# Gate projections moved among the SSD projections and kept in DRAM until their branch is merged

## The chip, the cores and the metric

The kernel runs on one core of one Trainium2 chip. The metric is device time in microseconds (us) of one launch, the median of several runs. The float32 products are made from three matmuls on rounded halves (high times high, high times low, low times high), so every weight block has to be split into a high and a low part before TensorE can use it.

## The reference, cut to what matters

Two layers, sequence of 512, model width 1024. What the change touches is one layer's mixing half:

```python
h = rmsnorm(x, norm_mix_g[l])
proj = h @ w_in[l]                      # 14384 columns: GLA, SSD, differential attention, 3 x 1024 gate logits
y_gla = gla_mixer(...)                  # 4 heads, chunked recurrence
y_ssm = ssd_mixer(z, xbc, dt, ...)      # 4 groups: conv of width 4 + silu on x, B, C; scan; y * silu(z); group rms norm
y_diff = diff_mixer(...)                # 8 heads, two softmaxes each
gates = sigmoid(gate_logits + b_gate).reshape(bsz, s_len, 3, D_MODEL)
mixed = gates[0] * (y_gla @ w_br_gla) + gates[1] * (y_ssm @ w_br_ssm) + gates[2] * (y_diff @ w_br_diff)
x = x + mixed @ w_out[l]
```

It is followed by a squared-ReLU MLP with 4096 hidden columns, a residual add, and after both layers a final norm.

## The kernel before, in words

All activations lie transposed, 128 channels on the partitions and 512 tokens in the free dimension. The unit of TensorE work is an *item*: one block of 128 output columns with all 1024 input channels (`item_a`, L867). It loads one weight block of 512 KB into a `wraw` tile (two buffers), splits it in two halves into `whi` (ScalarE copy) and `wlo` (VectorE or GpSimd subtraction), and issues 24 matmuls of 512 columns into one PSUM bank `d`. Then its `fin` takes the result from PSUM. `item_a2` (L893, for the SSD branch) gives two 128-column outputs from 512 channels, `item_w` (L942) a 512-column output with the tokens on the partitions; they are built of the same half blocks.

The order of the work is made at build time by a planner (`Flow`). Items stand in one list. `refill` (L373) keeps six half blocks queued: it walks the first `AHEAD` items of the list and takes the first whose buffers (`need`) and conditions (`cond`, `when`) are met on the planner's own clock. All the small work (scans, softmaxes, norms) is in *tasks*, generators that yield what they wait for; a ready task goes before the next matmul of an item. The planner's clock uses fixed costs per instruction (`Model.cost`, L153), and each engine's instructions, and the DMA issues of the one queue on SyncE (SP), are emitted in the order of that clock. On the chip each of these streams runs in order, so an instruction that waits holds what is behind it.

Items of a layer stand in the list in this order: the first pair of GLA heads; four SSD groups; the second pair of GLA heads; the SSD branch product of the last group; six `item_w` for the two halves of the differential attention; eight gates of the SSD branch; then per branch (GLA, then differential) gates and products interleaved, a gate two or four places ahead of its product; then the output projection and the MLP.

An SSD group (`ssd_group`, L1125) lists B, C, x0 to x3, z0 to z3. B, C and x go through `conv` (L1111): one ScalarE pass, three VectorE passes of 512 columns, a ScalarE tanh, one more VectorE pass. A z block costs one ScalarE and one VectorE pass. Then come the four `item_a2` that project the group before it (`ssm_part`, L1804). The group's tasks (`chunk`, `state`, `finish`) start when its convolutions are there; each `chunk` fetches decay rows from DRAM by the SP queue (`tw<-acs`, `tt<-acs`). `pj` has ten buffers and a group holds six.

A gate (`gate_item`, L1793) ends with one tanh from PSUM into a `tt` tile, which is held until the VectorE pass that multiplies it in. The SSD gates (`ssm_gates`, L1828) wait for the whole SSD sum, the others (`branch`, L1841) for a product that is so many places ahead.

Of the kernel before, what the change touches and what calls it, by code (L numbers as in the profile page):

```python
# [12 lines left out]
F32 = mybir.dt.float32  # L13
# [4 lines left out]
ALU = mybir.AluOpType  # L18
# [4 lines left out]
P = 128  # L23
S = 512
D = 1024
NT = S // P
KT = D // P
DEPTH = 2
# [6 lines left out]
O_Z, O_X, O_B, O_C, O_DT = 3088, 5136, 7184, 7696, 8208  # L35
O_CQ, O_CK, O_CV, O_GATE = 8240, 9264, 10288, 11312

C_CONVW, C_CONVB = 0, 96
C_MIX, C_MLP, C_BG, C_GK, C_DN, C_SN = 120, 128, 136, 160, 164, 165
N_COLS = 181  # L40

# [18 lines left out]


HOP = 0.22
SLACK, LAG, BACK, AHEAD = 0.4, 0.15, 6.0, 16
POOL_MARGIN = 0.5
QN = 6
LEAD = 2
# [584 lines left out]
class Trunk:  # L651
# [37 lines left out]
    def setup(self):  # L689
        nc, a, tc = self.nc, self.a, self.tc  # L690
        c = self.const
        self.ident = c.tile([P, P], F32, name="ident")
        make_identity(self.tc.nc, self.ident)
        self.ones = c.tile([P, P], F32R, name="one_row")
        self.one_row = self.ones.bitcast(F32)
        nc.gpsimd.memset(self.one_row, 1.0)
        self.xt_dram = [self.dram.tile([KT, P, S], F32, name=f"xt{l}") for l in range(DEPTH)]
        self.low_dram = [self.dram.tile([16, S], F32, name=f"low{l}") for l in range(DEPTH)]
        self.ac_dram = [self.dram.tile([32, S], F32, name=f"acs{l}") for l in range(DEPTH)]
        self.cols = [c.tile([P, N_COLS], F32, name=f"cols{l}") for l in range(DEPTH)]  # L700
        self.fcol = c.tile([P, KT], F32, name="fcol")
        self.masks = c.tile([P, 5, 16], U8, name="masks")
        self.ident32 = c.tile([P, 32], F32, name="ident32")
        self.cos = c.tile([P, NT, 8], F32, name="cos")
        self.sin = c.tile([P, NT, 8], F32, name="sin")
# [149 lines left out]
        self.act(hi, x, AF.Copy)  # L855
        self.sub(lo, x, hi)

    def item(self, blocks, start, body, fin, acts, cond, chain):
        def end(it):
            fin(it)  # L860
            acts.done()
        acts.users += 1
        it = Item(blocks, start, body, end, cond, acts.when, chain)
        self.f.items.append(it)
        return it
# [27 lines left out]
    def item_a2(self, w, k0, m0, acts, fin, extra=(), cond=()):  # L893
        f = self.f

        def body(it, i, wt):
            wh, wl = wt
            for j in range(2):
                k = i * 2 + j
                ah, al = acts.get(k)  # L900
                for u in range(2):
                    cs = slice(u * P, (u + 1) * P)
                    ps = it.held[u].ap
                    yield None
                    f.mm(ps, wh[:, j, cs], ah, k == 0, False)
                    f.mm(ps, wh[:, j, cs], al, False, False)
                    f.mm(ps, wl[:, j, cs], ah, False, k == 3)

        src = w[k0 * P:(k0 + 4) * P, m0 * P:(m0 + 2) * P]
        return self.item(Block(self, [src], 4, 256).parts(), [("d", ([P, 512],))] * 2 + list(extra),  # L910
                         body, fin, acts, cond, False)

    def item_pair(self, srcs, acts, fin):

# [207 lines left out]
        self.act(th, acc, AF.Tanh)  # L1122
        nc.vector.scalar_tensor_tensor(acc, th, 1.0, acc, op0=ALU.add, op1=ALU.mult)

    def ssd_group(self, l, g, h, evdt, quads, evy, before=None):  # L1125
        nc, a, f = self.nc, self.a, self.f
        w = a["w_in"][l]
        V, G = nc.vector, nc.gpsimd
# [15 lines left out]
                ev.t = f.at(it.held[1].ap)  # L1144
            self.item_a([w[:, c0:c0 + P]], h, fin, extra=pj, chain=False)

        conv_item(O_B + g * P, 16 + g, "b", st["evb"])
        conv_item(O_C + g * P, 20 + g, "c", st["evc"])
        for m in range(4):
            conv_item(O_X + g * 512 + m * P, g * 4 + m, m, st["evx"][m])  # L1150

        def z_item(m):
            def fin(it):
                if m % 2 == 0:
# [6 lines left out]
            c0 = O_Z + g * 512 + m * P  # L1161
            self.item_a([w[:, c0:c0 + P]], h, fin, extra=() if m % 2 else [("z4", ([P, 2, S],))],
                        cond=st["evz"][m - 1] if m % 2 else ())
        for m in range(4):
            z_item(m)

        def prep():
            yield ([st["evb"], st["evc"]] + ([before["evt"]] if before else []), {"m": 1, "tt": 4})
# [621 lines left out]
            f.spawn(head(hh))  # L1790


    def gate_item(self, l, br, m, h, cont, cond=()):  # L1793
        cb = C_BG + br * 8 + m

        def fin(it):
            ps, g = it.held
            self.act(g.ap, ps.ap, AF.Tanh, scale=0.5, bias=self.cols[l][:, cb:cb + 1])
            ps.free()
            cont(g)  # L1800
        self.item_a([self.a["w_in"][l][:, O_GATE + br * D + m * P:O_GATE + br * D + (m + 1) * P]], h, fin,
                    extra=[("tt", ([P, S],))], cond=cond).need["tt"] = 4

    def ssm_part(self, l, g, ev, quads, merged, evm):  # L1804
        V, f = self.nc.vector, self.f
        w = self.a["w_br_ssm"][l]
        acts = Acts(lambda j: self.part([quads[g]], j), last=lambda: self.drop([quads[g]]))
        left = [4]

        def fin_of(m0):  # L1810
            def fin(it):
                for i in range(2):
                    ps = it.held[i]
                    if g == 0:
                        merged[m0 + i] = it.held[2 + i]
                        self.act(merged[m0 + i].ap, ps.ap, AF.Copy)
                    else:
                        m = merged[m0 + i].ap
                        V.tensor_tensor(m, m, ps.ap, op=ALU.add)
                    ps.free()  # L1820
                left[0] -= 1
                if left[0] == 0:
                    evm.t = f.clock
            return fin
        for m0 in range(0, KT, 2):
            self.item_a2(w, g * 4, m0, acts, fin_of(m0), extra=[("res", ([P, S],))] * 2 if g == 0 else (), cond=ev)

    def ssm_gates(self, l, h, merged, evm, gated):  # L1828
        V, f = self.nc.vector, self.f

        def cont_of(m):
            def cont(g):
                x = merged[m].ap
                V.scalar_tensor_tensor(x, g.ap, 1.0, x, op0=ALU.add, op1=ALU.mult)
                g.free()
                gated[m].t = f.clock
            return cont
        for m in range(KT):
            self.gate_item(l, 1, m, h, cont_of(m), cond=evm)

    def branch(self, l, br, name, slots, evs, h, merged, gated, lead, final=None, gone=None):  # L1841
        V, f = self.nc.vector, self.f
        w = self.a[name][l]

        def drop():
            self.drop([s[0] for s in slots])
            if gone:
                gone.t = f.clock
        acts = Acts(lambda k: self.part([slots[k // 4][0]], k % 4),
                    last=drop)  # L1850
        made = [Event() for _ in range(KT)]
        taken = [Event() for _ in range(KT)]
        gs = [None] * KT

        def gate(m):
            def cont(g):
                gs[m] = g
                made[m].t = f.clock
            self.gate_item(l, br, m, h, cont, cond=taken[m - lead] if m >= lead else ())

        def prod(m):
            def fin(it):
                g = gs[m]
                V.scalar_tensor_tensor(g.ap, g.ap, 1.0, it.held[0].ap, op0=ALU.add, op1=ALU.mult)
                it.held[0].free()
                self.tt(merged[m].ap, merged[m].ap, g.ap, ALU.add)
                g.free()
                if final:
                    f.spawn(final(m))

            def hook(it):
                taken[m].t = f.clock
            it = self.item_a([w[:, m * P:(m + 1) * P]], acts, fin, cond=[*evs, made[m], gated[m]])
            it.hook = hook
        for m in range(KT + lead):
            if m < KT:
                gate(m)
            if m >= lead:
                prod(m - lead)


    def layer(self, l, ns, more):
# [22 lines left out]
                        lambda it: f.spawn(self.dt_task(l, it.held[0], evdt)), cols=48)  # L1905
        self.gla_duo(l, 0, h, gs[0], evg, dt_item)
        st = None
        for g in range(4):
            st = self.ssd_group(l, g, h, evdt, quads, evy[g], st)
            if g == 3 and l == 0:  # L1910
                late = Event()
                f.spawn(self.rope_tables(late))
                f.items[-1].hook = lambda it: setattr(late, "t", f.clock)
            if g > 0:
                self.ssm_part(l, g - 1, evy[g - 1], quads, merged, evm[g - 1])
        self.gla_duo(l, 1, h, gs[1], evg, before=[st["evt"]])
        self.ssm_part(l, 3, evy[3], quads, merged, evm[3])
        gone = Event()
        for duo in range(2):
            self.diff_duo(l, duo, h, ds[duo], evd[duo], gone if duo else None)  # L1920
        self.ssm_gates(l, h, merged, evm[3], gated)
        mq = [None, None]
        ma = Acts(lambda k: self.part(mq, k), [Event() for _ in range(KT)], lambda: self.drop(mq))

        def merge(m):
# [7 lines left out]
            nc.vector.scalar_tensor_tensor(lo, x.ap, 0.5, hi.bitcast(F32), op0=ALU.mult, op1=ALU.subtract)  # L1933
            x.free()
            ma.when[m].t = f.at(hi, lo)
        self.branch(l, 0, "w_br_gla", gs, evg, h, merged, gated, 2, gone=gone)
        self.branch(l, 2, "w_br_diff", ds, evd, h, merged, gated, 4, merge)
        cols = self.cols[l]
        n2 = Normed(self, cols[:, C_MLP:C_MLP + 8], 32, False)
        xn = n2.xs  # L1940
# [238 lines left out]
```

## Time and profile before

| | us |
|---|---|
| median of 3 runs (2815.11 to 2816.82) | 2815.18 |
| the profiled execution: its time | 2813.3 |
| the profiled execution: span of its instructions | 2811.4 |
| TensorE matmul busy | 2730.2 (97%) |
| VectorE busy | 1787.6 (64%) |
| ScalarE busy | 1313.6 (47%) |
| GpSimd busy | 560.9 (20%) |
| mean granted TensorE clock | 0.987 |

The chain of work that ended last is 89% TensorE and 6% VectorE. The span falls into stages that repeat in both layers: the first pair of GLA heads and the norm (to about 150 us), SSD groups with the second pair of GLA heads in their tail (about 200 to 650 and 1500 to 2000 us), differential attention with the GLA branch (650 to 950, 2000 to 2300), the differential branch and the output projection, and the MLP (1050 to 1400, 2430 to the end). Matmuls are pipelined, so a busy TensorE isn't a TensorE at its peak: the number of matmuls in a stretch says more than its busy time.

### The profile page before, as it was taken

Reading aid. Unit: us, or ns where it says so; the run is one execution under the profiler, and the core shown is the slowest. Engines: PE = TensorE matmul, PEld = TensorE weight load, DVE = VectorE, ACT = ScalarE, POOL = GpSimd, SP = SyncE. Lnnn points to the kernel's source line nnn. Section 1 sums busy time; section 2 is a strip of 40 time slices with the busy share of each in tenths; the row PEclk is TensorE's granted clock in tenths of the full one; section 3 lists DMA queues with packets and bytes.
Section 4 is the critical chain, followed back from the end, with each engine's and each line's share of the span. In section 5 each row is a group of like instructions: output and inputs, shape, how many; then the busy total and the mean of one; then the engine's idle time right before and its main releaser. Section 6 shows DMA issues by size and latency. Waiting matters only on the chain.

```text
span 2811.4 us, 40467 instructions
## 1 busy us (share of the span) xinstructions
PE 2730.2 (97%) x14956; PEld 2234.8 (79%) x14956; DVE 1787.6 (64%) x3804; ACT 1313.6 (47%) x2646; POOL 560.9 (20%) x620
## 2 busy tenths in 40 slices
PE   8998799999999999999999999899999999999998
PEld 6777587878888888888877778687888888888887
DVE  6787578864778455444478876778666754544445
ACT  5664545543656333223346656545365633332222
POOL 3323321331221001011013233333132100021001
PEclk9999899999999999999999999999999999999999
DMA  4343334223222343333343434332222233333332
GB/s 145 93 106 85 103 102 112 85 81 98 68 76 68 90 128 92 98 98 98 98 125 81 115 104 109 105 104 76 83 75 76 76 83 99 119 98 98 98 98 83
DMA packets 434818, 268.72 MB, mean 96 GB/s; under 512 B 15078, under 2 KB 407900, under 8 KB 434620
## 3 DMA queue, kind: packets, MB, share of 16 engines
q1 hardware_dynamic: 434004, 265.08, 33.7%
q8 instruction: 117, 1.92, 0.3%
q10 hardware_dynamic: 616, 1.06, 0.1%
q14 instruction: 81, 0.66, 0.1%
HBM read 259.62 MB, written 6.49 MB: 95 GB/s over the span
## 4 chain that ended last, share of the span: by engine, by line
PE 89%; DVE 6%; ACT 2%; DMA 1%; issue 1%; SPq 0%; DVEq 0%; ACTq 0%
PE d L367 79%; PE m L367 8%; PE m L371 3%; DVE tt L80 2%; DVE pj L80 1%; DVE wlo L80 1%; ACT tw L80 1%; DVE hl L80 1%; DVE rs_t L80 0%; ACT whi L80 0%; ACT cth L80 0%; DVE z L80 0%; DVE rs_y L80 0%; DMA z<-in_x 0%; DMA tt<-acs 0%
## 5 line engine op out<-in xcount | busy, mean ns | idle before, releaser
L367 PE MATMUL d<-hl,whi 128*128 128x512 f32 (+2 forms) x5696 | 1783.8, 395 | 24.4 <-ACT whi L80 19.6
L367 PEld LDWEIGHTS d<-hl,whi 128*128 128x128 f32 (+1 forms) x5696 | 1052.8, 189 | 240.0 <-ACT whi L80 22.5
L367 PE MATMUL d<-hl,wlo 128*128 128x512 f32 (+2 forms) x2848 | 1114.0, 391 | 15.4 <-DVE wlo L80 15.4
L80 ACT ACTIVATE whi<-wraw 128x512 fp32r<-128x512 f32 x868 | 541.0, 628 | 1050.6 <-PE d L367 958.2
L80 DVE TENSOR_TENSOR wlo<-wraw,whi 128x512 fp32r<-128x512 f32 (+1 forms) x807 | 587.7, 735 | 549.9 <-ACT whi L80 539.3
L367 PEld LDWEIGHTS d<-hl,wlo 128*128 128x128 f32 (+1 forms) x2848 | 536.8, 188 | 134.9 <-DVE wlo L80 21.2
L367 PE MATMUL d<-whi,hl 128*128 128x512 f32 x1280 | 410.8, 402 | 8.0 <-DVE z L80 5.8
L80 POOL TENSOR_TENSOR tt<-tt 128x512 f32<-128x512 f32 x128 | 159.5, 1255 | 983.9 <-ACT hl L80 857.1
L367 PEld LDWEIGHTS d<-whi,hl 128*128 128x128 f32 x1280 | 233.6, 190 | 55.2 <-DVE z L80 7.4
L367 PE MATMUL d<-wlo,hl 128*128 128x512 f32 x640 | 252.4, 394 | 0.0
L80 POOL TENSOR_TENSOR wlo<-wraw,whi 128x512 fp32r<-128x512 f32 (+1 forms) x61 | 79.5, 1304 | 360.0 <-ACT whi L80 255.7
L367 PEld LDWEIGHTS d<-wlo,hl 128*128 128x128 f32 x640 | 121.5, 190 | 26.7
L80 DVE TENSOR_TENSOR res<-res,d 128x512 f32<-128x512 f32 (+1 forms) x130 | 86.8, 675 | 73.6 <-PE d L367 73.5
L80 DVE SCALAR_TENSOR_TENSOR pj<-d,cols,pj 128x511 f32<-128x511 f32 (+1 forms) x144 | 106.7, 744 | 10.6 <-ACT pj L80 8.6
L80 POOL TENSOR_TENSOR tw<-tw,tt 128x1024 f32<-128x1024 f32 x32 | 77.2, 2415 | 102.4 <-ACT tw L80 85.2
L80 DVE SCALAR_TENSOR_TENSOR tt<-d,tt 128x512 f32<-128x512 f32 x64 | 44.0, 690 | 79.4 <-PE d L367 76.8
L80 ACT ACTIVATE tt<-m 128x512 f32<-128x512 f32 (+6 forms) x132 | 59.0, 451 | 74.9 <-PE m L367 48.2
L80 ACT ACTIVATE tt<-tt 128x256 f32<-128x256 f32 (+3 forms) x190 | 88.1, 498 | 12.0 <-DVE tt L80 9.6
L80 ACT ACTIVATE tw<-m,mx 128x512 f32<-128x512 f32 (+3 forms) x128 | 66.9, 525 | 34.0 <-DVE mx L80 33.0
L80 ACT ACTIVATE tw<-tw,acn 128x128 f32<-128x128 f32 x256 | 79.6, 388 | 5.0 <-DMA tw<-acs 5.0
L80 ACT ACTIVATE pj<-m 64x256 fp32r<-64x256 f32 (+1 forms) x160 | 66.4, 420 | 31.5 <-DVE pj L80 14.7
L367 PEld LDWEIGHTS m<-z,tt 128*128 128x128 f32 x488 | 69.3, 190 | 7.7 <-DVE tt L80 0.4
(181 smaller groups left out, 2477.2 us busy)
## 6 DMA issues: line engine op xcount, KB each, us to landing
wraw<-in_w_in SPq DMA_DIRECT2D x224, 512.0 KB
wraw<-in_w_mlp_up SPq DMA_DIRECT2D x64, 512.0 KB
wraw<-in_w_mlp_down SPq DMA_DIRECT2D x64, 512.0 KB
tw<-acs SPq DMA_DIRECT2D x32, 512.0 KB
wraw<-in_w_br_ssm SPq DMA_DIRECT2D x32, 512.0 KB
wraw<-in_w_br_gla SPq DMA_DIRECT2D x16, 512.0 KB
wraw<-in_w_br_diff SPq DMA_DIRECT2D x16, 512.0 KB
wraw<-in_w_out SPq DMA_DIRECT2D x16, 512.0 KB
```

The source lines that it names most:

```text
L80: fn = lambda a=args, k=kw: real(*a, **k)
L367: self.model.post(self.clock - c, lambda: self.nc.tensor.matmul(out, lhsT, rhs, start=start, stop=stop))
L371: self.model.post(self.clock - 0.109, lambda: self.nc.tensor.transpose(out, in_, ident))
```

## The change

Every gate block becomes an item without a condition. Its tanh is stored to a DRAM tensor (`gate_dram`, 24 blocks of 256 KB for a layer) and its `tt` tile is freed. The eight SSD gates stand two to a group among the x and z blocks; the other sixteen stand behind the differential attention's projections, ahead of all branch products. A product loads its gate back when it is queued (`hook`); the SSD gates are loaded back and multiplied in by a task when the SSD sum is done. In a group, x and z blocks alternate and B and C stand in the middle. The planner looks 28 items ahead in place of 16.

```diff
+PATTERN = ["x0 z0 x1 z1 b g c z2 x2 z3 x3 g"] * 4
-SLACK, LAG, BACK, AHEAD = 0.4, 0.15, 6.0, 16
+SLACK, LAG, BACK, AHEAD = 0.4, 0.15, 6.0, 28
...
+        self.gate_dram = [self.dram.tile([3 * KT, P, S], F32, name=f"gates{l}") for l in range(DEPTH)]
...
-        conv_item(O_B + g * P, 16 + g, "b", st["evb"])
-        conv_item(O_C + g * P, 20 + g, "c", st["evc"])
-        for m in range(4):
-            conv_item(O_X + g * 512 + m * P, g * 4 + m, m, st["evx"][m])
...
-        for m in range(4):
-            z_item(m)
+        for what in PATTERN[g].split():
+            m = int(what[1:] or 0)
...
+            elif what == "g":
+                next(gates, lambda: None)()
...
+        for p in parts:
+            p()
...
-    def gate_item(self, l, br, m, h, cont, cond=()):
+    def gate_item(self, l, br, m, h, ev):
...
             self.act(g.ap, ps.ap, AF.Tanh, scale=0.5, bias=self.cols[l][:, cb:cb + 1])
             ps.free()
-            cont(g)
-                    extra=[("tt", ([P, S],))], cond=cond).need["tt"] = 4
+            nc.sync.dma_start(self.gate_dram[l][br * KT + m], g.ap)
+            g.free()
+            ev.t = self.f.at(self.gate_dram[l][br * KT + m])
+        self.item_a([self.a["w_in"][l][:, c0:c0 + P]], h, fin, extra=[("tt", ([P, S],))]).need["tt"] = 3
...
+    def ssm_gates(self, l, merged, evm, evg, gated):
         for m in range(KT):
-            self.gate_item(l, 1, m, h, cont_of(m), cond=evm)
+            yield (evm, evg[m], {"tt": 3})
+            g = self.T("tt")
+            self.nc.sync.dma_start(g.ap, self.gate_dram[l][KT + m])
+            yield f.at(g.ap)
+            x = merged[m].ap
+            V.scalar_tensor_tensor(x, g.ap, 1.0, x, op0=ALU.add, op1=ALU.mult)
...
             def hook(it):
-                taken[m].t = f.clock
-            it = self.item_a([w[:, m * P:(m + 1) * P]], acts, fin, cond=[*evs, made[m], gated[m]])
+                self.nc.sync.dma_start(it.held[1].ap, self.gate_dram[l][br * KT + m])
+            it = self.item_a([w[:, m * P:(m + 1) * P]], acts, fin, extra=[("tt", ([P, S],))],
+                             cond=[*evs, evg[m], gated[m]])
...
-        for m in range(KT + lead):
-            if m < KT:
-                gate(m)
-            if m >= lead:
-                prod(m - lead)
+        for m in range(KT):
+            prod(m)
...
+        gates = iter([lambda br=br, m=m: self.gate_item(l, br, m, h, evgt[br][m])
+                      for br in (1, 0, 2) for m in range(KT)])
...
+        for g in gates:
+            g()
+        f.spawn(self.ssm_gates(l, merged, evm[3], evgt[1], gated))
```

## Rows read from the trace of the kernel before

**Rows 1.** Busy time by stretch, in order: PE, PEld, DVE, ACT, POOL; granted clock, DMA.
```profile
200.00:650.00 450.00, 418.05 (x2562) 335.24 (x2562) 329.11 (x700) 230.43 (x465) 126.48 (x129) 0.96 0.35 96
350.00:450.00 100.00, 100.00 (x539) 81.98 (x538) 75.29 (x138) 50.48 (x100) 20.24 (x23) 1.00 0.40 108
650.00:950.00 300.00, 300.00 (x1532) 252.22 (x1531) 199.72 (x563) 162.18 (x384) 51.11 (x84) 1.00 0.28 77
1500.00:2000.00 500.00, 478.43 (x3235) 383.80 (x3234) 388.43 (x791) 278.81 (x584) 153.44 (x141) 0.98 0.36 98
```

**Rows 2.** The same view for PE's matmuls into `d` alone (busy, count).
```profile
200.00:650.00 450.00, 363.78 (x1475) 0.96 0.35 96
350.00:450.00 100.00, 89.39 (x380) 1.00 0.40 108
650.00:950.00 300.00, 259.83 (x1042) 1.00 0.28 77
...
1150.00:1200.00 50.00, 50.00 (x222) 1.00 0.34 95
...
1500.00:2000.00 500.00, 411.17 (x1650) 0.98 0.36 98
```

**Rows 3.** The same view for PE's matmuls into `m` alone.
```profile
200.00:650.00 450.00, 75.48 (x1087) 0.96 0.35 96
350.00:450.00 100.00, 14.79 (x159) 1.00 0.40 108
650.00:950.00 300.00, 77.34 (x490) 1.00 0.28 77
1500.00:2000.00 500.00, 95.10 (x1585) 0.98 0.36 98
```

**Rows 4.** Waits of PE: total us, times, longest.
```profile
PE d L367 <- ACT whi L80: 19.6, 6, 11.0
```

**Rows 5.** Timeline of the SP queue, 240 to 300 us: start, length, issue.
```profile
251.40 0.59 SPq L80 DMA_DIRECT2D tt<-acs  x1
278.06 0.37 SPq L80 DMA_DIRECT2D tw<-acs  x1
...
279.17 2.50 SPq L80 DMA_DIRECT2D wraw<-in_w_in  x2
```

**Rows 6.** Costliest groups, shapes kept apart: busy us, mean ns, idle before.
```profile
L80 DVE TENSOR_TENSOR wlo<-wraw,whi 128x512 fp32r<-128x512 f32 x804 | 586.7, 736 | 548.2 <-ACT whi L80 537.6 <-PE d L367 9.4
L80 DVE SCALAR_TENSOR_TENSOR pj<-cth,pj 128x512 f32<-128x512 f32 x48 | 38.3, 798 | 10.5 <-ACT cth L80 10.1
L80 DVE SCALAR_TENSOR_TENSOR pj<-d,cols,pj 128x511 f32<-128x511 f32 x48 | 35.5, 742 | 8.6 <-ACT pj L80 8.6
```

**Rows 7.** Instructions on the tensor `xt`: ns min/median/max, first and last start.
```profile
L80 SPq DMA_DIRECT2D xt<-res x16: 421/467/1246, 35.9 to 1448.6; - x16
L80 SPq DMA_DIRECT2D res<-xt x16: 320/574/784, 996.7 to 2415.7; - x16
```

**Rows 8.** Busy time by stretch, as in rows 1, in the output projection.
```profile
1000.00:1050.00 50.00, 50.00 (x223) 41.40 (x222) 27.04 (x42) 19.33 (x32) 0.00 (x0) 1.00 0.43 132
```

**Rows 9.** Groups in 457 to 833.3, 833.3 to 930.5 (two) and 1850 to 2285.6 us (two).
```profile
L80 ACT ACTIVATE tt<-d,cols 128x512 f32<-128x512 f32 x10 | 6.8, 680 | 3.5 <-PE d L367 3.4
...
L80 ACT ACTIVATE tt<-d,cols 128x512 f32<-128x512 f32 x7 | 4.8, 684 | 5.8 <-PE d L367 5.8
L80 DVE SCALAR_TENSOR_TENSOR tt<-tt,d 128x512 f32<-128x512 f32 x6 | 4.1, 684 | 1.2 <-PE d L367 1.2
...
L80 ACT ACTIVATE tt<-d,cols 128x512 f32<-128x512 f32 x15 | 10.2, 683 | 6.5 <-PE d L367 6.4
L80 DVE SCALAR_TENSOR_TENSOR tt<-tt,d 128x512 f32<-128x512 f32 x3 | 2.0, 681 | 0.1
```

**Rows 10.** PE's matmuls into `m` between layer 0's last attention projection and its last head.
```profile
833.30:930.50 97.20, 32.97 (x206) 1.00 0.26 71
```

**Rows 11.** Timeline of ACT: the last head's result is taken from PSUM.
```profile
929.69 0.69 ACT L80 ACTIVATE z<-m,dcol 128x512 f32<-128x512 f32 x1 [2.08 <-PE m L371]
```

More of the change, by code (lines that the diff above doesn't have):

```diff
@@ L856, in split, with item @@
         self.sub(lo, x, hi)
-    def item(self, blocks, start, body, fin, acts, cond, chain):
+    def item(self, blocks, start, body, fin, acts, cond, chain, count=1):
         def end(it):
@@ L861, in end @@
             acts.done()
-        acts.users += 1
+        acts.users += count
         it = Item(blocks, start, body, end, cond, acts.when, chain)
@@ L910, in item_a2 @@
         return self.item(Block(self, [src], 4, 256).parts(), [("d", ([P, 512],))] * 2 + list(extra),
-                         body, fin, acts, cond, False)
+                         body, fin, acts, cond, False, 0)
     def item_pair(self, srcs, acts, fin):
@@ L1123, in conv, with ssd_group @@
         nc.vector.scalar_tensor_tensor(acc, th, 1.0, acc, op0=ALU.add, op1=ALU.mult)
-    def ssd_group(self, l, g, h, evdt, quads, evy, before=None):
+    def ssd_group(self, l, g, h, evdt, quads, evy, before, gates, parts):
         nc, a, f = self.nc, self.a, self.f
@@ L1163, in z_item @@
                         cond=st["evz"][m - 1] if m % 2 else ())
-        for m in range(4):
-            z_item(m)
+        parts = iter(parts)
+        for what in PATTERN[g].split():
+            m = int(what[1:] or 0)
+            if what == "b":
+                conv_item(O_B + g * P, 16 + g, "b", st["evb"])
+            elif what == "c":
+                conv_item(O_C + g * P, 20 + g, "c", st["evc"])
+            elif what[0] == "x":
+                conv_item(O_X + g * 512 + m * P, g * 4 + m, m, st["evx"][m])
+            elif what[0] == "z":
+                z_item(m)
+            elif what == "g":
+                next(gates, lambda: None)()
+            elif what == "p":
+                next(parts, lambda: None)()
+        for p in parts:
+            p()
         def prep():
@@ L1790, in diff_duo @@
             f.spawn(head(hh))
-    def gate_item(self, l, br, m, h, cont, cond=()):
+    def gate_item(self, l, br, m, h, ev):
+        nc = self.nc
         cb = C_BG + br * 8 + m
@@ L1799, in fin @@
             ps.free()
-            cont(g)
-        self.item_a([self.a["w_in"][l][:, O_GATE + br * D + m * P:O_GATE + br * D + (m + 1) * P]], h, fin,
-                    extra=[("tt", ([P, S],))], cond=cond).need["tt"] = 4
+            nc.sync.dma_start(self.gate_dram[l][br * KT + m], g.ap)
+            g.free()
+            ev.t = self.f.at(self.gate_dram[l][br * KT + m])
+        c0 = O_GATE + br * D + m * P
+        self.item_a([self.a["w_in"][l][:, c0:c0 + P]], h, fin, extra=[("tt", ([P, S],))]).need["tt"] = 3
     def ssm_part(self, l, g, ev, quads, merged, evm):
@@ L1824, in fin_of, with branch @@
             return fin
-        for m0 in range(0, KT, 2):
-            self.item_a2(w, g * 4, m0, acts, fin_of(m0), extra=[("res", ([P, S],))] * 2 if g == 0 else (), cond=ev)
-    def ssm_gates(self, l, h, merged, evm, gated):
-        V, f = self.nc.vector, self.f
[L1831 to L1837, printed above, removed]
-        for m in range(KT):
-            self.gate_item(l, 1, m, h, cont_of(m), cond=evm)
-    def branch(self, l, br, name, slots, evs, h, merged, gated, lead, final=None, gone=None):
+        acts.users = 4
+        return [lambda m0=m0: self.item_a2(w, g * 4, m0, acts, fin_of(m0),
+                                           extra=[("res", ([P, S],))] * 2 if g == 0 else (), cond=ev)
+                for m0 in range(0, KT, 2)]
+    def ssm_gates(self, l, merged, evm, evg, gated):
+        V, f = self.nc.vector, self.f
+        for m in range(KT):
+            yield (evm, evg[m], {"tt": 3})
[4 more added lines that the diff above has]
+            V.scalar_tensor_tensor(x, g.ap, 1.0, x, op0=ALU.add, op1=ALU.mult)
+            g.free()
+            gated[m].t = f.clock
+    def branch(self, l, br, name, slots, evs, merged, gated, evg, final=None, gone=None):
         V, f = self.nc.vector, self.f
@@ L1850, in branch @@
                     last=drop)
[L1851 to L1859, printed above, removed]
         def prod(m):
             def fin(it):
-                g = gs[m]
+                g = it.held[1]
                 V.scalar_tensor_tensor(g.ap, g.ap, 1.0, it.held[0].ap, op0=ALU.add, op1=ALU.mult)
@@ L1871, in hook @@
             def hook(it):
-                taken[m].t = f.clock
-            it = self.item_a([w[:, m * P:(m + 1) * P]], acts, fin, cond=[*evs, made[m], gated[m]])
+                self.nc.sync.dma_start(it.held[1].ap, self.gate_dram[l][br * KT + m])
+            it = self.item_a([w[:, m * P:(m + 1) * P]], acts, fin, extra=[("tt", ([P, S],))],
+                             cond=[*evs, evg[m], gated[m]])
             it.hook = hook
-        for m in range(KT + lead):
-            if m < KT:
-                gate(m)
-            if m >= lead:
-                prod(m - lead)
+            it.cond0 = evg[m]
+        for m in range(KT):
+            prod(m)
     def layer(self, l, ns, more):
@@ L1907, in layer @@
         st = None
+        evgt = [[Event() for _ in range(KT)] for _ in range(3)]
+        gates = iter([lambda br=br, m=m: self.gate_item(l, br, m, h, evgt[br][m])
+                      for br in (1, 0, 2) for m in range(KT)])
         for g in range(4):
-            st = self.ssd_group(l, g, h, evdt, quads, evy[g], st)
+            st = self.ssd_group(l, g, h, evdt, quads, evy[g], st, gates,
+                                self.ssm_part(l, g - 1, evy[g - 1], quads, merged, evm[g - 1]) if g else ())
             if g == 3 and l == 0:
@@ L1913, in layer @@
                 f.items[-1].hook = lambda it: setattr(late, "t", f.clock)
-            if g > 0:
-                self.ssm_part(l, g - 1, evy[g - 1], quads, merged, evm[g - 1])
         self.gla_duo(l, 1, h, gs[1], evg, before=[st["evt"]])
-        self.ssm_part(l, 3, evy[3], quads, merged, evm[3])
+        for p in self.ssm_part(l, 3, evy[3], quads, merged, evm[3]):
+            p()
         gone = Event()
@@ L1920, in layer @@
             self.diff_duo(l, duo, h, ds[duo], evd[duo], gone if duo else None)
-        self.ssm_gates(l, h, merged, evm[3], gated)
+        for g in gates:
+            g()
+        f.spawn(self.ssm_gates(l, merged, evm[3], evgt[1], gated))
         mq = [None, None]
@@ L1935, in merge @@
             ma.when[m].t = f.at(hi, lo)
-        self.branch(l, 0, "w_br_gla", gs, evg, h, merged, gated, 2, gone=gone)
-        self.branch(l, 2, "w_br_diff", ds, evd, h, merged, gated, 4, merge)
+        self.branch(l, 0, "w_br_gla", gs, evg, merged, gated, evgt[0], gone=gone)
+        self.branch(l, 2, "w_br_diff", ds, evd, merged, gated, evgt[2], merge)
         cols = self.cols[l]
```

## The prediction

> **What bounds the kernel now.** I read the stretches of the span first, then what PE did in each, then its waits. PE is busy for all of 650 to 950 us and for 418 of 450 and 478 of 500 us in the two SSD stages [rows 1], so the kernel is bound by TensorE, and what can be won is the time in which TensorE isn't running matmuls at full rate. Busy time hides part of that, so I count matmuls. In the MLP a window of 50 us holds 222 matmuls of 512 columns [rows 2], or 0.2252 us each; a gate, 24 of them, is 5.4 us. In 650 to 950 us the 1042 big matmuls [rows 2] need 234.7 us, which leaves 65.3 us for the small ones, whose busy time reads 77.34 us [rows 3]: as PE loses nothing there, small matmuls are worth 0.845 of what they read. With these two prices:
>
> - 200 to 650 us: 1475 x 0.2252 + 75.48 x 0.845 = 332.2 + 63.8 = 396.0 us of need in 450: 54.0 us lost.
> - 1500 to 2000 us: 1650 x 0.2252 + 95.10 x 0.845 = 371.6 + 80.4 = 452.0 in 500: 48.0 us lost.
> - 350 to 450 us, inside the first: 85.6 + 12.5 = 98.1 in 100: 1.9 us lost [rows 2, 3].
>
> So 102 us are lost in two stages that need 848. PE is idle for 32.0 and 21.6 us of it [rows 1]; the granted clock, 0.96 and 0.98 of the full 2.4 GHz, is worth about 18 + 10 us more; the rest is matmuls that come late one by one. The longest single stall is 11.0 us, for a weight's high half [rows 4]. It follows a hold on the SP queue: after a decay row was issued at 251.40 us the next issue comes at 278.06, and two weight loads stand right behind it [rows 5].
>
> What is scarce in these stages is VectorE. It is busy for 329.11 + 388.43 = 717.5 us [rows 1], 84.6% of PE's need, where the stretch of 350 to 450 us, with 75.29 of 98.1, stands at 76.7%. A convolution block asks it for three passes of 0.742, one of 0.798 and two weight subtractions of 0.736 us [rows 6], 4.5 of its own 5.4 us of PE; a gate for the two subtractions alone, 1.5 us. Six convolutions in a row leave the scan tasks nearly no VectorE time.
>
> **The change part by part.** *Eight gates move into the groups of each layer.* The work is the same: 24 matmuls, two splits, one tanh, later one VectorE pass. In the SSD stages PE's need grows by 16 x 5.4 = 86.5 us to 934.5, VectorE's by 16 x 2 x 0.736 = 23.6 to 741.1 us, so its share falls to 79.3%. The loss is 12.0% of need at a share of 84.6% and 1.9% at 76.7%, or 1.28% a point; at 79.3% the line gives 5.2%, 49 us in place of 102: a gain of 53 us. One end is no gain: 650 to 950 shows that a stage can run with no loss, or with much, at like shares, and coincidences may count more than shares. The other is the quiet stretch's 1.9% throughout, a loss of 18 and a gain of 84 us. I take 53, nearer to the quiet row, as the new share is.
>
> *x and z alternate, B and C in the middle.* No instruction is added. Two convolutions are no longer neighbours, except where B and C surround a gate, so the share above also holds over a few items and not only as a mean; I count that inside the 53 us. A group's tasks start later, since x3 is its eleventh block and not its sixth; PE has the next group's blocks to fill this, but the last group has not (below).
>
> *Stores and reloads.* 24 stores and 24 reloads of 256 KB a layer are new on SP. The residual's transfers have that size: 0.467 and 0.574 us of SP each [rows 7], 25 us a layer. SP only issues, and in the output projection, where a reload goes with every block, PE is busy for all 50 us and makes 223 matmuls at a DMA share of 0.43 [rows 8]. I take nothing for them. What hides the reload is the queue of six half blocks, some 13 us, between it and the product's end; without that cover each of 48 would add its landing time.
>
> The store adds a wait: SP stands until the tanh is done, with the next weight loads behind it. Between nothing (the planner places it behind the tanh) and one hold like that at 251 us for each group, 8 x 11.0 = 88 us, I take nothing: a store waits for a tanh one item old, the held issue waited for a buffer that the late VectorE had to free. The Trainium skill, "DMA: Bandwidth & Descriptors", section "Anatomy of one DMA", says that a DMA engine never waits on a semaphore; the wait happens on the issuing sequencer before dispatch. By that rule the sum would be the rival of the SP holds below, and the trace's gap from 251.40 to 278.06 us agrees with the rule.
>
> *The cover of the attention shrinks.* Gates and GLA products fill PE while the attention heads' chain runs. Until layer 0's last head is out at 929.69 us [rows 11], 10 + 7 gates and 6 products have been used; in layer 1, until 2285.6 us, 15 and 3 [rows 9]. After the change 16 gates and 8 products are left for this, 24 for 23 and for 18. Behind x3 of the last group there used to stand four z blocks, now one gate: three items less. Layer 0 is then two items short, 2 x 5.4 = 11 us of stall, and layer 1 has three to spare. Ends: nothing, and the rival below; I take 11 us.
>
> *28 items of lookahead* lets these sixteen gates be reached from the second GLA pair on; its price is in the same rival. The wait between the last GLA product and the first differential one stays, as there is no filler for it before or after.
>
> Sum: -53 + 11 = -42 us. The profiled execution took 2813.3 us for its span of 2811.4, so 2771.3; it is 1.9 us below the median of the runs, so on the median 2815.2 - 42 = 2773 us.
>
> **The rivals.** *The stages go quiet.* If spacing the convolutions, and not the mean share, is what 350 to 450 us shows, the gain is 84 us: 2731. Against it: those 100 us have light scan work, and the loss elsewhere comes where scans and convolutions meet.
>
> *It does not do what it says.* The order on the chip is the planner's, from ready times, and the list only proposes. If holds like that at 251 us come from scans alone, the gain is 0, with 0 to 11 us for the cover: 2815 to 2826. For it: the stalls sit in few places; against it: the share falls whatever the order.
>
> *The cover runs out.* With 28 items in view and no condition, all sixteen gates may be taken before the last attention projection. Then 97.2 us of heads have 0.845 x 32.97 = 27.9 us of small matmuls [rows 10] and eight products, 43.2 us, to run beside them: 26 us idle, and as much in layer 1 by estimate. In 200 to 650 us 32 us of idle time went with 18 us of clock, so each idle us costs 1.56: 81 us, and -53 + 81 = +28: 2843, slower. It turns the sign once over 34 us are idle, some six items short in both layers together. For it: layer 0 has but one filler to spare. Against it: a gate is taken early only where PE would have been idle, and there are few such places between 450 and 830 us.
>
> *Stores hold the SP queue.* One hold of 11.0 us in each of eight groups: -42 + 88 = +46: 2861, slower. It decides when a store's tanh runs later than the planner thinks by more than a weight's lead of two blocks. For it: the hold at 251 us; against it: ScalarE is far from full, 230 of 450 us [rows 1].
>
> **How the numbers follow.** The forecast, 2773 with a range of its own of 2745 to 2800, has 0.56; the quiet stages 0.11; no effect 0.15; the cover 0.10; the SP holds 0.08. A measurement of this kernel can tell a change of over 0.2%, 5.6 us, from none. Faster: 0.56 + 0.11 + 0.02 from the upper side of no effect = 0.69. Same: 0.08 of no effect and 0.01 of the SP holds = 0.09. Slower: 0.05 + 0.10 + 0.07 = 0.22. The range reaches from 2735, into the quiet case, to 2832, past no effect and into the cover: about 0.05 is left below it and 0.13 above.
>
> **What would show it.** Right: in the SSD stages of the changed kernel the loss counted as above is near 50 us, the 11 us stall at the first group is gone, VectorE stands near 79% of PE's need, and PE stays at full clock in most windows. The MLP windows still hold 222 matmuls. A few us of idle PE appear before layer 0's differential products and none in layer 1. Wrong: SSD stages that lose 90 us or more; SP waiting for ACT for tens of us; idle windows with many tasks waiting after the last attention projection.

## The result and the profile after

The changed kernel takes 2773.9 us (median of 4 runs, 2772.4 to 2776.7) against 2815.1 us: a ratio of 0.9857, with a 95% interval of 0.9842 to 0.9871. The forecast was 2773. The profiled execution has a span of 2770.7 us, 40.7 less.

The same views as before the prediction, now of the changed kernel. Its SSD stage in layer 0 lasts to about 700 us, since gates have moved into it, so the windows here and in all comparisons below are 200 to 700 and 1450 to 2000 us. First all engines (PE, PEld, DVE, ACT, POOL, granted clock, DMA):

```profile
200.00:700.00 500.00, 480.30 (x2875) 388.55 (x2874) 352.38 (x751) 260.81 (x529) 144.19 (x139) 0.98 0.39 109
1450.00:2000.00 550.00, 539.91 (x3586) 437.90 (x3586) 411.41 (x843) 311.93 (x644) 168.49 (x151) 1.00 0.40 110
700.00:1000.00 300.00, 298.34 (x1516) 251.00 (x1515) 204.50 (x533) 161.71 (x377) 54.57 (x85) 1.00 0.36 105
```

Then PE's matmuls into `d` alone:

```profile
200.00:700.00 500.00, 424.77 (x1739) 0.98 0.39 109
1450.00:2000.00 550.00, 474.07 (x1957) 1.00 0.40 110
700.00:1000.00 300.00, 260.65 (x1052) 1.00 0.36 105
...
1150.00:1200.00 50.00, 50.00 (x223) 1.00 0.33 95
```

And those into `m`:

```profile
200.00:700.00 500.00, 81.24 (x1136) 0.98 0.39 109
1450.00:2000.00 550.00, 95.60 (x1629) 1.00 0.40 110
700.00:1000.00 300.00, 72.26 (x464) 1.00 0.36 105
```

With the prediction's two prices, 0.2252 us a big matmul and 0.845 of what small ones read, layer 0's stage now needs 1739 x 0.2252 + 81.24 x 0.845 = 460.3 of 500 us and loses 39.7; layer 1's needs 521.5 of 550 and loses 28.5. The kernel before, counted in these windows, lost 54.4 and 50.8 us. So 37 of the 41 us come from the two stages: 15 from layer 0, 22 from layer 1. The attention stage, 700 to 1000 us, loses 300 - 298.0 = 2.0 us (counted with a price of small matmuls that takes 650 to 950 us of the kernel before as free of loss), and the MLP's window holds 223 matmuls for 222 [rows 2].

PE's longest waits after the change (total, times, longest); [rows 4] is their counterpart:

```profile
PE d L368 <- DVE z L81: 13.0, 6, 4.1
PE d L368 <- ACT whi L81: 9.3, 3, 3.7
PE d L368 <- DVE wlo L81: 8.8, 5, 2.0
```

The 11.0 us wait for a weight is gone. The list is now headed by PE's wait for VectorE to write `z` tiles, which before came to 7.2 us:

```profile
PE d L367 <- DVE z L80: 7.2, 7, 2.4
```

Its longest, 4.1 us, is for a value block of the second GLA pair. SP's wait for the tanh is large in sum, and below it are the stores and reloads (ns min, median, max):

```profile
SPq L81 <- ACT tt L81: 180.2, 41, 11.4
```
```profile
L81 SPq DMA_DIRECT2D gates<-tt x48: 319/338/986, 130.4 to 2267.3; - x48
L81 SPq DMA_DIRECT2D tt<-gates x48: 319/464/910, 663.7 to 2330.9; - x48
```

The order, from the stores, is as the change says: in each layer eight gates lie in the groups, up to 493 and 1845 us, and sixteen after 660 and 2020 us.

### The profile page after: what moved, and what is told of

The parts are those of the page before. It is cut to its first block, busy times and chain, and to the rows that moved or that the text cites. A ratio compares the mean times of both kernels' runs of the same rounds, so it can differ in the third digit from the quotient of the medians.

```text
span 2770.7 us, 40678 instructions
## 1 busy us (share of the span) xinstructions
PE 2714.3 (98%) x14956; PEld 2228.9 (80%) x14956; DVE 1774.5 (64%) x3803; ACT 1310.6 (47%) x2646; POOL 571.1 (21%) x621
## 5 line engine op out<-in xcount | busy, mean ns | idle before, releaser
L81 DVE TENSOR_TENSOR wlo<-wraw,whi 128x512 fp32r<-128x512 f32 x807 | 589.7, 737 | 472.2 <-ACT whi L81 462.5
L81 POOL TENSOR_TENSOR tt<-tt 128x512 f32<-128x512 f32 (+1 forms) x129 | 162.1, 1267 | 949.6 <-ACT hl L81 768.5
L81 ACT ACTIVATE tt<-m 128x512 f32<-128x512 f32 (+5 forms) x132 | 58.9, 452 | 62.1 <-PE m L368 33.7
L81 DVE TENSOR_TENSOR tt<-tt,pj 128x256 f32<-128x256 f32 (+1 forms) x124 | 67.5, 583 | 29.8 <-ACT tt L81 29.6
L81 ACT ACTIVATE tw<-tw,acn 128x128 f32<-128x128 f32 x256 | 79.8, 388 | 2.2 <-DMA tw<-acs 2.2
```

The source lines that it names most:

```text
L81: fn = lambda a=args, k=kw: real(*a, **k)
```

## The experiments

Ratios are to the kernel before, run on the same chip, with 95% intervals. "Share" is VectorE's busy time over PE's need, "lost" the time of the window less PE's need, both counted as above; layer 0 is 200 to 700 us, layer 1 1450 to 2000.

| kernel | gates in groups, order, lookahead | us | ratio | share, lost in layer 0 | in layer 1 |
|---|---|---|---|---|---|
| before | none, old, 16 | 2815.1 | 1 | 79.2%, 54.4 | 85.0%, 50.8 |
| e1 | none, old, 16, DRAM copies | 2821.0 | 1.0021 (1.0012 to 1.0031) | 78.2%, 61.0 | 85.5%, 51.2 |
| e2 | none, new, 16 | 2820.9 | 1.0022 (1.0013 to 1.0031) | 79.8%, 57.9 | 83.0%, 52.3 |
| e4 | none, old, 28 | 2799.1 | 0.9944 (0.9927 to 0.9961) | 76.6%, 31.5 | 82.0%, 59.8 |
| e6 | none, new, 28 | 2815.0 | 1.0002 (0.9992 to 1.0011) | 79.9%, 49.1 | 78.9%, 38.5 |
| e3 | two, old, 16 | 2779.1 | 0.9874 (0.9859 to 0.9889) | 76.7%, 30.8 | 77.8%, 31.5 |
| e5 | two, new, 16 | 2776.4 | 0.9866 (0.9850 to 0.9883) | 75.9%, 40.5 | 78.4%, 27.1 |
| e7 | two, old, 28 | 2778.2 | 0.9871 (0.9856 to 0.9886) | 76.7%, 31.1 | 78.1%, 33.4 |
| after | two, new, 28 | 2773.9 | 0.9857 (0.9842 to 0.9871) | 76.6%, 39.7 | 78.9%, 28.5 |
| e8 | before, a conv pass less | 2791.1 | 0.9914 (0.9899 to 0.9929) | 76.4%, 47.6 | 78.3%, 32.9 |
| e9 | after, VectorE work added | 2787.0 | 0.9906 (0.9891 to 0.9921) | 80.3%, 35.5 | 82.5%, 47.7 |
| e11 | three, new, 28 | 2783.0 | 0.9889 (0.9874 to 0.9904) | 78.8%, 36.6 | 77.9%, 29.3 |
| e10 | four, new, 28 | 2837.3 | 1.0083 (1.0067 to 1.0100) | 74.2%, 27.1 | 74.1%, 29.3 |
| e12 | after, stores on ACT's queue | 2775.5 | 0.9862 (0.9847 to 0.9877) | 76.5%, 40.1 | 78.7%, 28.4 |

**e1 to e4: the parts one by one.** All have the DRAM copies. e1 has nothing else:

```diff
-PATTERN = ["x0 z0 x1 z1 b g c z2 x2 z3 x3 g"] * 4
+PATTERN = ["b c x0 x1 x2 x3 z0 z1 z2 z3"] * 4
-SLACK, LAG, BACK, AHEAD = 0.4, 0.15, 6.0, 28
+SLACK, LAG, BACK, AHEAD = 0.4, 0.15, 6.0, 16
```

> The DRAM copies alone: all 24 gates of a layer stand behind the attention projections, stored and loaded back, groups in their old order (B, C, x0 to x3, z0 to z3), lookahead 16. If VectorE's share in the SSD stages decides (the theory of the prediction), nothing there changes: about 2815 us, within 6 us. If spacing of the convolutions decides: the same, 2815. If stores on the SP queue hold weight loads, slower than 2830. If any reordering by the planner moves the stalls at random: anywhere from 2780 to 2840.

e2 has `x0 z0 x1 z1 b c z2 x2 z3 x3` and 16.

> As the run before with x and z blocks alternating and B and C in the middle, but no gate in a group, lookahead 16. Share theory: VectorE still has 84 to 85% of PE's need in the SSD stages, so little, 2805 to 2820 us. Spacing theory: most of the gain, 2775 to 2790.

e3 has `b c x0 x1 x2 x3 g z0 z1 z2 z3 g` and 16.

> Old order of the group with the two gates added, one behind x3 and one behind z3, lookahead 16. Share theory: most of the gain of 41 us, 2770 to 2785 us. Spacing theory: six convolutions still stand in a row, so 2800 to 2820.

e4 is e1 with 28.

> As the first run with a lookahead of 28 in place of 16 and nothing else. Share theory: the gates can be reached a little earlier, but not in the groups: 2805 to 2820 us. If the lookahead itself is the cause (gates fill the stalls of the SSD stages from their place at the list's end): 2775 to 2790.

The copies and the gates' place behind the attention cost 6 us. The new order adds nothing. Gates in the groups, in the old order, take 42 us off e1: the whole effect. The lookahead alone takes 22 us off e1, which lies between its two expectations and which the prediction had at nothing. It puts no gate into the groups, but it changes the planner's order enough that the one long hold of the first group is gone. PE's waits from 200 to 350 us, in e1:

```profile
PE d L368 <- ACT whi L81: 10.9, 1, 10.9
PE m L368 <- DVE tt L81: 8.3, 3, 4.7
PE d L368 <- ACT res L81: 3.4, 1, 3.4
```

and in e4, all of them:

```profile
PE d L368 <- ACT res L81: 2.1, 1, 2.1
PE m L372 <- DVE pj L81: 1.6, 1, 1.6
PE m L368 <- DVE tt L81: 0.2, 1, 0.2
```

In e1 SP stands still from a decay row at 251.76 to the next at 279.21 us, with the weight loads behind, as before [rows 5]; in e4 it issues weights through that time:

```profile
251.76 0.58 SPq L81 DMA_DIRECT2D tt<-acs  x1
279.21 0.37 SPq L81 DMA_DIRECT2D tw<-acs  x1
```
```profile
246.01 30.97 SPq L81 DMA_DIRECT2D wraw<-in_w_in  x6
```

The profile puts SP's gap in e1 down to PE, for 26.8 us (SP's waits from 240 to 300 us; in the kernel before, 26.0):

```profile
SPq L81 <- PE m L368: 27.3, 2, 26.8
```

The decay tile `tw` can be filled again once PE's small matmuls have read it. In the kernel before these start at 276.79 us, after PE has waited 2.41 us for VectorE, which has worked with hardly a pause since 257.13.

In layer 1 e4 loses 59.8 us, 9 more than before. A stall of some 20 us in layer 0 thus comes and goes with details of the order, and with gates in the groups it is gone too.

**e5 to e7: two parts at a time.** The same two lines are edited.

> The changed kernel with a lookahead of 16 in place of 28: gates in the groups and the new order. If gates in the groups carry the gain and lookahead adds little to them: 2773 to 2783 us. If lookahead adds what it added without gates in the groups (22 us): 2790 to 2800.

> The new order with a lookahead of 28, no gate in a group. Share theory: as the lookahead alone, 2794 to 2804 us. If spacing works only once the planner sees further: under 2785.

> The old order with the gates in the groups and a lookahead of 28, so the changed kernel without its new order. Share theory: as the changed kernel within 6 us, 2768 to 2780. If order matters once gates are there: 2785 or more.

With gates in the groups every order and lookahead gives 2774 to 2779 us; the intervals of e3, e5, e7 and the changed kernel overlap. The stages behind that total differ more: with the old order layer 0 loses 31 us and the stretch from 2000 to 2400 us 11 to 12, with the new one 40 and 3. Without gates in the groups, order and lookahead together give back 16 of the 22 us that lookahead alone won (e6 against e4), and e6 misses both of its expectations. Of what was expected only the loose alternative of e1, that any reordering moves the stalls, covers this; with gates in the groups the total hardly depends on the order.

**e8 and e9: is it VectorE's share?** e8 takes VectorE work away and moves no gate:

```diff
-        for sh in (1, 2, 3):
+        for sh in (1, 2):
```

> The kernel before with one of the convolution's three shifted VectorE passes left out (48 passes of 0.746 us over both layers, 36 us of VectorE; the output lacks that tap). No gate is moved. Share theory: VectorE falls from 84.6 to 80.4% of PE's need in the SSD stages, a loss of 56 in place of 102 us there, so 2765 to 2780. If gates help by something other than VectorE's load: 2805 to 2818.

e9 gives the moved gates VectorE work:

```diff
+            if br == 1:
+                for _ in range(4):
+                    nc.vector.scalar_tensor_tensor(g.ap, g.ap, 1.0, g.ap, op0=ALU.mult, op1=ALU.max)
             nc.sync.dma_start(self.gate_dram[l][br * KT + m], g.ap)
```

> The changed kernel with four extra VectorE passes of 512 columns, each leaving its data as it is, behind the tanh of every SSD gate: 16 x 4 x 0.69 = 44 us of VectorE in the SSD stages, which puts its share of PE's need back from 79 to about 84%. Share theory: the gain goes, 2803 to 2818 us. If the gates help as PE work between the convolutions, whatever VectorE has to do: 2772 to 2785.

Both move the time the way the share theory says, and both land between their two expectations: e8 wins 24 us where the theory had 35 to 50, and e9 loses 13 where it had 29 to 44, 2 us outside the other expectation. By layers it is clearer. In layer 1 e8 alone takes 18 us off the loss, where the change takes 22, and e9 gives back 19. Order and lookahead move that loss too, from 38.5 to 59.8 us without gates in the groups and from 27.1 to 33.4 with two; e8's 32.9 lies below the first range and e9's 47.7 above the second. e9's rows from 1450 to 2000 us, all engines, then `d`, then `m` (1879 x 0.2252 + 93.71 x 0.845 = 502.3 of 550):

```profile
1450.00:2000.00 550.00, 526.78 (x3395) 423.95 (x3395) 414.66 (x816) 302.72 (x622) 160.23 (x149) 0.98 0.37 104
```
```profile
1450.00:2000.00 550.00, 461.43 (x1879) 0.98 0.37 104
```
```profile
1450.00:2000.00 550.00, 93.71 (x1516) 0.98 0.37 104
```

In the table's last column share and loss go together: eight kernels with a share from 74 to 79% lose 27 to 33 us (a ninth, e6, 38.5), and five with 82 to 86% lose 48 to 60. It isn't the prediction's line: e10, at 74%, loses as much as the changed kernel at 79%. Nor does it show that the share sets the loss. The share's divisor is the window less the loss, so of two kernels with the same VectorE time the one that loses more shows the higher share: in e4 and e3 VectorE is busy for 401.9 and 403.3 of layer 1's 550 us, and they lose 59.8 and 31.5. Only e8 and e9, which edit VectorE's work itself, bear on the cause, and after either edit the planner lays out all work anew.

The stalls in e9 point to another engine as well. Of its 47.7 us 16.8 lie in 1625 to 1650 and 1850 to 1875 us, around its two longest waits of PE in this stage, 5.45 and 3.53 us. At the second, ScalarE works through decay exponentials (`tw<-tw,acn`) with the tanh that frees PE's bank (`tt<-d,cols`) behind them, and VectorE is idle for 5.22 us, waiting for ScalarE too (lines of three engines):

```profile
1850.88 2.44 ACT L81 ACTIVATE tw<-tw,acn 128x128 f32<-128x128 f32 x8
1854.32 2.44 ACT L81 ACTIVATE tw<-tw,acn 128x128 f32<-128x128 f32 x8
1858.55 2.32 DVE L81 SCALAR_TENSOR_TENSOR pj<-d,cols,pj 128x511 f32<-128x511 f32 x3 [5.22 <-ACT pj L81]
1859.45 0.67 ACT L81 ACTIVATE tt<-d,cols 128x512 f32<-128x512 f32 x1
1860.18 0.73 PE L368 MATMUL d<-hl,whi 128*128 128x512 f32 x2 [3.53 <-ACT tt L81]
```

The kernel before has the like in layer 1, where weight copies stand behind such exponentials; there ScalarE had itself waited 1.27 and 2.49 us for VectorE a few us earlier:

```profile
1651.21 0.74 PE L367 MATMUL d<-hl,whi 128*128 128x512 f32 x2 [2.27 <-ACT whi L80]
1813.39 1.03 PE L367 MATMUL d<-hl,whi 128*128 128x512 f32 x2 [3.49 <-ACT whi L80]
```

No run takes work off ScalarE or moves its exponentials alone, so how much of layer 1's loss is VectorE's load and how much ScalarE's order is open. In layer 0 the share does not order the losses (e9 loses 35.5 at 80.3%, e8 47.6 at 76.4%); there e9's extra VectorE work cost nothing (35.5 us lost against 39.7). What decides in layer 0 beyond the hold that e4 removed was not settled.

**e10 and e11: how long the cover lasts.** Four gates in a group, `x0 z0 g x1 z1 b g c z2 g x2 z3 x3 g`, and three, `x0 z0 g x1 z1 b g c z2 x2 z3 x3 g`.

> Four gates to an SSD group in place of two, so sixteen of 24 stand in the groups. Share theory: VectorE falls to about 75%, another 25 to 30 us off the loss in the SSD stages. Cover theory: only eight gates and eight products are left beside the attention heads, some seven items short in layer 0 and two in layer 1: about 50 us idle there, with the clock 60 to 80. Together 2795 to 2825; if cover doesn't matter, 2745.

> Three gates to a group. Share theory: 12 to 15 us off the loss in the SSD stages; cover theory: three items short in layer 0, none in layer 1: 16 to 25 us lost there. Together 2768 to 2785; if cover doesn't matter, 2760.

e10 is clearly slower than the kernel before, and 12 us above its expectation. Its SSD stages lose 56 us in place of 68, but from 700 to 1000 us PE runs out of work (all engines, `d`, `m`: 900 x 0.2252 + 81.32 x 0.845 = 271.4 of 300):

```profile
700.00:1000.00 300.00, 279.70 (x1390) 232.12 (x1389) 198.74 (x563) 152.69 (x368) 55.17 (x85) 0.96 0.30 90
```
```profile
700.00:1000.00 300.00, 225.03 (x900) 0.96 0.30 90
```
```profile
700.00:1000.00 300.00, 81.32 (x490) 0.96 0.30 90
```

28.6 us are lost there in place of 2.0, and 42.9 in place of 2.9 from 2000 to 2400 us: 67 us together. All eight gates left for the attention are stored by 819.06 us, before the weights of its last projection are issued at 870.40. From 940.7 to 977.5 us PE's timeline shows only attention matmuls (into `m`), with waits for VectorE or ScalarE between them, and the first differential product behind them. Three of its lines:

```profile
969.46 1.11 PE L372 MATMUL m<-ident,tt 128*128 128x128 f32 x4 [2.57 <-DVE tt L81]
974.46 1.12 PE L372 MATMUL m<-ident,tt 128*128 128x128 f32 x4 [3.89 <-DVE tt L81]
977.54 1.22 PE L368 MATMUL d<-hl,whi 128*128 128x512 f32 x2 [1.96 <-ACT whi L81]
```

e11 shows the edge. Its third gate takes 2 us off the SSD stages, where 12 to 15 were expected, and with twelve gates and eight products left it loses 9.5 us from 700 to 1000 us (`d`, then `m`: 229.0 + 61.5 of 300), against 2.0 with sixteen gates:

```profile
700.00:1000.00 300.00, 254.46 (x1017) 0.98 0.34 101
```
```profile
700.00:1000.00 300.00, 72.76 (x464) 0.98 0.34 101
```

**e12: stores on another queue.**

```diff
-            nc.sync.dma_start(self.gate_dram[l][br * KT + m], g.ap)
+            nc.scalar.dma_start(self.gate_dram[l][br * KT + m], g.ap)
```

> The changed kernel with the gates' stores issued from ScalarE's queue in place of SP's, so that no weight load stands behind a tanh. If SP's waits for the tanh (180 us in all in the changed kernel) delay weights: 2755 to 2768 us. If they are hidden by the two weight buffers, as the prediction took them: 2770 to 2780.

2775.5 us, and the stage losses are the same within half a microsecond. SP's 180 us of waiting for tanhs cost no time.

No run was faster than the changed kernel.

## Why the prediction came out right

**The counting held.** The loss lay in the two SSD stages and 37 of the 41 us came from them; MLP and attention stages are as they were. That 650 to 950 us ran without loss was assumed to fix the price of small matmuls, so it can't also show, as the prediction has it, that a stage runs without loss at a like share; and that stretch's share, 199.72 of 300 us, is 67%, not 84.6%.

**The main term was too large.** The line through the shares gave 53 us; these stages gave 37. Its lower end, the quiet stretch's 1.9% loss at 76.7%, is no property of the share: e10 loses 27 + 29 us at 74%. And at the upper end layer 0's mean hid a hold that has more to do with the order (e4). That the gates in the groups bring the gain is shown (e3 against e1). The mechanism given for it, that light blocks relieve a VectorE that is near PE's need, is supported in layer 1 by two edits that move the loss both ways (e8, e9), with ScalarE's part untested, and is not shown for layer 0. That the held issue at 251 us waited for the late VectorE is right only at one remove: it waited for PE's matmuls, and these for VectorE.

**The cover's 11 us did not come, where it was put.** In the changed kernel the last head of layer 0 leaves PSUM here:

```profile
951.26 0.69 ACT L81 ACTIVATE z<-m,dcol 128x512 f32<-128x512 f32 x1 [2.69 <-PE m L372]
```

The last GLA products were still running, and 24 fillers just sufficed. PE is busy throughout the 21 us before, and waits 1.66 us once behind it, at 961.51, for a weight's low half:

```profile
930.00:951.00 21.00, 21.00 (x108) 17.60 (x106) 17.24 (x44) 5.96 (x11) 2.44 (x2) 1.00 0.33 101
```

This fits the count of 23 and not the three items taken off for the missing z blocks. Instead the later tasks of the last group met the second GLA pair: PE waits 4.1 us for VectorE's pass over that pair's values, which in VectorE's order stands behind a scan and the start of the group's norm:

```profile
566.66 1.22 PE L368 MATMUL d<-whi,hl 128*128 128x512 f32 x2 [4.10 <-DVE z L81]
567.68 0.63 PE L368 MATMUL d<-wlo,hl 128*128 128x512 f32 x1
568.11 1.05 PE L368 MATMUL d<-whi,hl 128*128 128x512 f32 x2
568.97 0.63 PE L368 MATMUL d<-wlo,hl 128*128 128x512 f32 x1
```

So a main term 16 us too large and a cost of 11 us that was not there, with some 4 us won elsewhere, left the sum within 1 us: the total is better than its parts, and that is luck.

**The prices of nothing.** Stores and reloads: right (e12), and the rival of the held SP queue falls: SP waits 180 us for tanhs, and PE doesn't lose by it. The Trainium skill's "DMA: Bandwidth & Descriptors", in "Anatomy of one DMA" (a section on GpSimd's path), has semaphore waits happen on the issuing sequencer before dispatch. SP's 180 us agree with that. Order: counted inside the 53 us, worth 4 us at most (e7), which the intervals don't tell from nothing. Lookahead: worth nothing once the gates are in the groups (e5), as priced; on its own it moved the time by 22 us, which was not seen.

**The rival of the cover** was the right one to fear, for a neighbour of this change. It forecast 2843 us for all gates taken before the last attention projection, with eight products left beside the heads. e10, which moves eight more gates into the groups, meets that condition in layer 0 and measures 2837: PE is idle for 20.3 us there (26 had been worked out), and the attention stages of both layers lose 67 us more than the changed kernel's (81).

**The signs.** The first group's stall is gone, the MLP's window is as it was, and VectorE stands at 77.8% of PE's need over both stages (79 had been forecast), but the loss left there is 68 us and not near 50. One sign of being wrong, SP waiting for ScalarE for tens of us, came with 180 us and meant nothing.

## What to carry to other kernels

Count matmuls against a stretch that runs at full rate before believing a busy share: here PE was 97% busy over the whole, and 95% in the two stages that lost 105 us, about 50 more than its idle time there. Work that loads little but the bound engine can be worth more between blocks that load its helpers, but it is also cover for stages of dependent small steps later on, and it can be spent once: two gates a group won 41 us, four lost 24. And where an order comes from a planner, test a part alone and in company: the lookahead's 22 us and the order's loss of 16 both vanish once the gates are in the groups.

## What the runs showed that was not expected

After PE's idle 4.1 us above, three matmuls of 512 columns take 567.68 to 568.97 us, about 0.43 us each in place of 0.2252. The granted clock is half of the full one there, the lower of the two levels, 1.2 GHz, so a stall costs more than its length (all engines, clock, DMA):

```profile
567.00:571.00 4.00, 4.00 (x10) 3.13 (x10) 3.76 (x14) 0.89 (x2) 0.00 (x0) 0.50 0.25 45
```

In layer 1 every kernel with gates in the groups still loses 27 us or more, whatever their number and the order; no run here removed that.
